# Projection order in a one-layer hybrid decoder step: the fourth delta-net head's columns before the last four gate blocks

## The chip, the cores and the metric

One core of one Trainium2 chip runs the whole step as a single program. The metric is the device time of one execution in microseconds; a comparison takes the median of several runs. Five engines work in parallel, each through its own list of instructions in order: TensorE (PE, with its weight loads shown apart as PEld), VectorE (DVE), ScalarE (ACT), GpSimd (POOL) and SyncE (SP). DMAs are issued by SP and by ACT, from the same in-order lists as their other work.

## What is computed

A hybrid decoder layer for a prompt of 1024 tokens and, beside it, 8 sample tokens with 4096 cached positions each. One input projection (1024 columns of x against 5648 columns of weights) feeds three branches, and a gate:

```python
proj = jnp.dot(h, w['in'])
q_a, k_a, v_a, xbc, dt_raw, qkv_c, beta_raw, a_raw, z = jnp.split(proj, idx, axis=-1)
z_a, z_b, z_c = jnp.split(z, [D_A, D_A + D_B], axis=-1)
...
o_a = (rms_norm(o_a) * w['subln'] * (1 - lam_init)).reshape(b, L, D_A) * jax.nn.silu(z_a)
...
qkv, conv1 = causal_conv(qkv, conv0, conv_w)      # gated delta net, 4 heads of 128
qkv = jax.nn.silu(qkv).astype(f32)
...
o, S1 = gated_delta_chunked(q, k, v, g, beta, S0.astype(f32))
o = (rms_norm(o) * norm_g).reshape(b, L, D_C).astype(z.dtype) * jax.nn.silu(z)
...
out = jnp.dot(jnp.concatenate([o_a, o_b, o_c], axis=-1), w['out'])
```

The branches are differential attention (4 heads), a Mamba-2 scan (SSD) and a gated delta net (4 heads, chunks with a triangular solve each). Everything is float32; the projections are done as three products of rounded high and low parts.

## The kernel before

The projection is feature-major: `proj_fm` (lines 424 to 467) takes a list of items, one for each block of 128 columns. An item is 72 matmuls (three groups `n` of 344 tokens, 24 matmuls each, line 458) into one of three PSUM banks "pj"; after each group the item's `sink` empties the bank. Four kinds of item matter here. A `z_item` (line 980) is a gate block: ACT copies each group into a buffer (line 991), and after every second block both are put through SiLU on ACT and written to DRAM (line 986), to be read again much later. A `g_item` (line 1572) is a third of a delta-net head (its q, its k or its v): `conv_item` (line 953) empties the bank with four DVE operations per group (lines 964 and 969), and after the head's third item the SiLU of all three is recorded and the three buffers are appended to `graw[h]`. An `x_item` does the same for the SSD branch, and a `v_item` is an attention value block.

`groups[3]` (line 1588) lists the 33 items that run in the long middle stretch: four v, head 1's three, four x, head 2's three, four x, twelve z, and last head 3's three. Each long-lived result sits in the pool `up` of 12 buffers of 4 KB per partition (`unit`, line 136): the convolved q, k and v of a head, the z buffers, and inside `gdn_head` the tiles kN, vb, LT, AT, Dm, kb and oC; also attention's kTh (two) and vh.

`gdn_head` (line 1035) is one head: sums of squares, transposes, decay and score blocks for eight chunks (lines 1102 to 1119, the "front"); then the inversion: LT is written to DRAM and read back as Dm by DMAs on ACT's queue (lines 1122 to 1127), 31 dependent pairs of DVE steps (lines 1136 to 1140), the result written and read back again (lines 1143 to 1147); then products and eight sequential state steps (lines 1208 to 1228), and the store. `gdn_all` (line 1601) runs the four heads in turn and yields 0.5 at a time while a head's three buffers are not yet there.

`drive` (line 280) interleaves generators while the program is written: it always advances the one that is furthest behind in its share, by the costs that they yield. The middle stretch is four such drives, cut after 9, 18, 30 and 33 items (`CUTS`); `take` gives the delta net 77% of its cost (`GF`) over them, in proportion to the items. Attention's first loads (`attention_begin`, line 673) are recorded before the last cut's three items. Then the weight pools are closed, and a final `drive` (line 1736) interleaves attention, the rest of the delta net, the SSD scan, the sample steps, the rest of the paged sample attention and the first output weights. The output projection (line 1824) comes last. The program is then scheduled by priority in this recorded order, with the delta net's instructions put forward by 50 places (`OFF`).

Of the kernel before, what the change touches and what calls it, by code (L numbers as in the profile page):

```python
# [87 lines left out]
def trunk_kernel(  # L88
# [47 lines left out]
    def unit(shape, dt=F32, n="u"):  # L136
        return up.tile(shape, dt, tag="u", name=nm(n))
# [807 lines left out]
    def silu_flush():  # L945
        for y, bias, done in late_silu:
            i = act(y, y, AF.Silu, bias=bias)
        exp_ln_tables(i)
        for y, bias, done in late_silu:
            done(y)  # L950
        late_silu.clear()

    def conv_item(c0, wb, ws, ti, tj, done, flush, silu_bias=0.0):
        wv = [vec[:, wb + i * ws + ti:wb + i * ws + ti + 1] for i in range(4)]
        cur = [None]

        def sink(n, ps):
            if n == 0:
                cur[0] = unit([P, T], n="cy")
            y = cur[0]  # L960
            o = 3 if n else 0
            m = CH if n < 2 else CH - NS
            c0_ = n * CH
            V.tensor_scalar_mul(y[:, c0_:c0_ + m], ps[:, o:o + m], wv[3])
            for i in range(3):
                s_ = 0 if n else 3 - i
                q = o - 3 + i + s_
                yv = y[:, c0_ + s_:c0_ + m]
                stt(yv, ps[:, q:q + m - s_], wv[i], yv, ALU.mult, ALU.add)
            if n == 2:  # L970
                V.tensor_copy(tail[:, tj, :], ps[:, o + m - 3:o + m + NS])
                late_silu.append((y, silu_bias, done))
                if flush:
                    silu_flush()

        return (c0, sink, 3)
# [3 lines left out]
    def z_item(j):  # L980

        cur = [None]

        def done(y):
            V.tensor_copy(zS[:, j, :], y[:, T:NTOK])
            S.dma_start(out=zfd[j], in_=y[:, 0:T])

        def sink(n, ps):
            if n == 0:
                cur[0] = unit([P, NTOK], n="zf")  # L990
            S.copy(cur[0][:, n * CH:(n + 1) * CH], ps)
            if n == 2:
                late_silu.append((cur[0], 0.0, done))
                if j % 2:
                    silu_flush()

        return (CZ + j * P, sink, 0)
# [574 lines left out]
    def g_item(h, j):  # L1572
        def done(y):
            graw.setdefault(h, []).append(y)

        return conv_item(CG + 512 * j + h * P, 56, 12, 4 * j + h, 8 + 4 * j + h, done, j == 2)

    def x_item(i):
        def done(y):
            S.dma_start(out=yxd[i], in_=y)  # L1580

        return conv_item(CX + i * P, 16, 8, i, i, done, i % 2 == 1, vec[:, 48 + i:49 + i])
# [4 lines left out]
        [g_item(0, j) for j in range(3)],  # L1587
        [v_item(h) for h in range(4)] + [g_item(1, j) for j in range(3)]
        + [x_item(i) for i in range(4)] + [g_item(2, j) for j in range(3)]
        + [x_item(i) for i in range(4, 8)] + [z_item(j) for j in (4, 5, 6, 7, 0, 1, 2, 3, 8, 9, 10, 11)]  # L1590
        + [g_item(3, j) for j in range(3)],
    ]
    fg = proj_fm([i for g in groups for i in g], lead_w)

# [340 lines left out]
```

## Time and profile before

| | |
|---|---|
| three runs | 1270.9, 1263.82, 1271.76 us; median 1270.9 |
| the profiled execution | 1265.4 us, span 1262.6 us |
| PE busy, weight loads | 1130.7 us (90%), 951.7 us (75%) |
| DVE, ACT, POOL busy | 816.4 us (65%), 477.3 us (38%), 640.6 us (51%) |
| mean granted TensorE clock | 0.951 of full |
| last projection matmul (line 458) | about 839 us |
| first output-projection matmul in a row (line 1824) | 1102 us |

The busy shares are means over stretches with different limits. The middle stretch of projections ends near 839 us, the mixed stretch of the final `drive` lasts from there to about 1092 us, and the output projection takes the rest. The profile's matmul ends are modelled, so PE's busy time and that of its weight loads are both shown.

### The profile page before, as it was taken

What the parts mean: (1) busy time and instruction counts of PE and PEld (TensorE: products, weight loads), DVE (VectorE), ACT (ScalarE), POOL (GpSimd) and SP (SyncE); (2) the same over time, 40 slices, a digit from 0 to 9 for tenths busy, and PEclk for the clock granted to TensorE, in tenths of its full rate; (3) what the DMA queues carried; (4) which work ended last, traced back from release to release, by engine and by line L of the source; (5) the groups of instructions that cost most, each with busy time, mean ns of one, the idle gap of its engine ahead of it and who ended that gap; (6) DMA issues with size and microseconds to landing.
All of it is one profiled execution on the core that took longest, in us unless ns stands there. A gap on an engine that the chain in (4) does not pass through costs nothing.

```text
span 1262.6 us, 22284 instructions
## 1 busy us (share of the span) xinstructions
PE 1130.7 (90%) x7365; PEld 951.7 (75%) x7365; DVE 816.4 (65%) x1945; ACT 477.3 (38%) x1003; POOL 640.6 (51%) x778
## 2 busy tenths in 40 slices
PE   4999999988789989979897899978898999699997
PEld 3799888777668869759776788857577778678876
DVE  5723596538568669953564935786778888664444
ACT  6333224201213532223353243436548658341111
POOL 3757867734567674573865788860023241241100
PEclk9999899998879999999898899989899999899999
DMA  8756676993786882794896699999786564951320
GB/s 287 213 165 194 225 216 195 354 314 94 234 309 218 275 276 81 227 347 155 283 322 204 191 339 330 315 306 228 196 231 187 127 168 137 303 193 63 123 70 34
DMA packets 246451, 275.56 MB, mean 218 GB/s; under 512 B 31905, under 2 KB 163376, under 8 KB 246322
## 3 DMA queue, kind: packets, MB, share of 16 engines
q1 hardware_dynamic: 168082, 214.44, 52.6%
q10 hardware_dynamic: 78256, 59.72, 16.5%
q8 instruction: 58, 0.95, 0.3%
q14 instruction: 55, 0.45, 0.1%
HBM read 231.59 MB, written 42.67 MB: 217 GB/s over the span
## 4 chain that ended last, share of the span: by engine, by line
PE 50%; DVE 17%; DMA 17%; ACT 5%; issue 4%; POOL 3%; SPq 2%; ACTq 1%; DVEq 0%; POOLq 0%
PE b L458 22%; PE b L1824 10%; DVE U L159 4%; PE pv L886 3%; DMA vt<-in_cache_v_dram 3%; DMA w<-in_w_in_dram 3%; DVE cy L167 2%; DVE lg L841 2%; DMA kt<-in_cache_k_dram 2%; POOL kt L840 2%; DMA Dm<-invd 1%; PE b L745 1%; DMA invd<-U 1%; DVE e L721 1%; ACT e L156 1%
## 5 line engine op out<-in xcount | busy, mean ns | idle before, releaser
L458 PE MATMUL b<-hh,whi 128*128 128x344 f32 (+1 forms) x2016 | 506.2, 334 | 22.8 <-DVE cy L167 13.8
L840 POOL TENSOR_TENSOR kt<-kt,qb 128x256 f32<-128x256 f32 x512 | 361.7, 740 | 144.9 <-DMA kt<-in_cache_k_dram 108.7
L458 PEld LDWEIGHTS b<-hh,whi 128*128 128x128 f32 x2016 | 360.2, 195 | 53.8 <-issue 27.7
L458 PE MATMUL b<-hh,wlo 128*128 128x344 f32 (+1 forms) x1008 | 330.7, 333 | 3.5 <-POOL wlo L201 3.4
L841 DVE TENSOR_REDUCE lg<-kt 128x16 f32<-128x1024 f32 x128 | 154.7, 1212 | 95.4 <-POOL kt L840 88.6
L458 PEld LDWEIGHTS b<-hh,wlo 128*128 128x128 f32 x1008 | 196.1, 196 | 15.5 <-issue 10.1
L201 POOL TENSOR_TENSOR wlo<-w,whi 128x512 fp32r<-128x512 f32 x86 | 110.9, 1293 | 89.8 <-ACT whi L155 89.1
L1824 PE MATMUL b<-wo,mh 128*128 128x512 f32 (+1 forms) x408 | 121.8, 380 | 0.0
L155 ACT ACTIVATE whi<-w 128x512 fp32r<-128x512 f32 x86 | 53.8, 630 | 132.6 <-PE b L458 86.7
L167 DVE SCALAR_TENSOR_TENSOR cy<-b,vec,cy 128x341 f32<-128x341 f32 (+4 forms) x180 | 98.9, 564 | 1.3
L886 PE MATMUL pv<-vt,wz 128*32 128x512 f32 x512 | 80.9, 648 | 10.4 <-DMA vt<-in_cache_v_dram 8.5
L1824 PEld LDWEIGHTS b<-wo,mh 128*128 128x128 f32 x408 | 74.7, 188 | 14.1
L1792 POOL TENSOR_TENSOR ml<-zt,mh 128x512 fp32r<-128x512 f32 x16 | 22.4, 1400 | 109.0 <-ACT mh L1791 93.4
L1824 PE MATMUL b<-wo,ml 128*128 128x512 f32 (+1 forms) x204 | 77.2, 378 | 0.0
L155 ACT ACT_TABLE_LOAD x37 | 47.5, 1283 | 26.7 <-POOL wlo L201 7.8
L159 DVE TENSOR_TENSOR U<-U,Dm 128x60 f32<-128x60 f32 (+24 forms) x124 | 43.5, 351 | 17.3 <-DMA Dm<-invd 15.2
L156 ACT ACTIVATE e<-e,nmx 128x128 f32<-128x128 f32 (+7 forms) x64 | 49.1, 768 | 6.7 <-DMA ql<-qfd 2.8
L718 PE MATMUL b<-kTh,qh 128*128 128x128 f32 (+3 forms) x96 | 39.9, 422 | 9.2 <-DVE mx L721 7.2
L159 DVE TENSOR_TENSOR y<-b,gate 128x512 f32<-128x512 f32 (+1 forms) x17 | 11.1, 659 | 54.1 <-PE b L1824 54.1
L1824 PEld LDWEIGHTS b<-wo,ml 128*128 128x128 f32 x204 | 38.4, 188 | 7.3
L159 DVE TENSOR_TENSOR U<-U 128x60 f32<-128x60 f32 (+24 forms) x124 | 41.4, 334 | 2.3
L745 PE MATMUL b<-vh,wT 128*128 128x128 f32 x288 | 40.3, 285 | 1.0 <-ACT wT L738 0.6
(524 smaller groups left out, 1957.2 us busy)
## 6 DMA issues: line engine op xcount, KB each, us to landing
kt<-in_cache_k_dram SPq DMA_DIRECT2D x256, 256.0 KB
vt<-in_cache_v_dram SPq DMA_DIRECT2D x256, 256.0 KB
w<-in_w_in_dram ACTq DMA_DIRECT2D x82, 256.0 KB
zfd<-zf ACTq DMA_DIRECT2D x12, 512.0 KB
wo<-in_w_out_dram SPq DMA_DIRECT2D x12, 512.0 KB
om<-mixd SPq DMA_DIRECT2D x24, 256.0 KB
xt<-in_x_prompt_dram SPq DMA_DIRECT2D x8, 512.0 KB
hx<-in_w_ada_dram SPq DMA_DIRECT2D x16, 256.0 KB
```

The lines of the kernel that those rows point to most:

```text
L155: return S.activation(out, in_, func, bias=bias, scale=scale)
L156: return S.activation(out, in_, func, bias=bias, scale=scale, accum_out=accum)
L159: return V.tensor_tensor(out=out, in0=a, in1=b, op=op)
L167: return V.scalar_tensor_tensor(out=out, in0=a, scalar=s, in1=b, op0=op0, op1=op1)
L201: G.tensor_tensor(out=lo, in0=w32, in1=hi.bitcast(F32), op=ALU.subtract)
L458: TE.matmul(ps[:, 0:N], a, b[k][:, sl], start=(i == 0), stop=(i == 23))
L718: TE.matmul(ps[:, 0:b - a], qh[:, m, ts], kT[m][:, a:b], start=True, stop=False)
L745: TE.matmul(po[:, 0:P], wTs[j // 4][:, j % 4, :], vh[:, j, :], start=(j == 0), stop=(j == i))
L840: G.tensor_tensor(out=kt[:, j, c], in0=kt[:, j, c], in1=qb[:, c], op=ALU.mult)
L841: V.tensor_reduce(out=lg[:, 2 * g:2 * g + 2, :], in_=kt.rearrange("p j (a d) -> p j a d", d=64), axis=AX.X, op=ALU.add)
L886: mm = TE.matmul(pv[32 * r:32 * r + 32, :], wz[:, 2 * g + j, :], vt[:, j, :], start=(b == 0 and g < 2), stop=(b == NS - 1 and g >= 14 and ...
L1824: TE.matmul(ps[c], m[a][:, kt % 4, :], w[kt][:, c[0]:c[1]], start=(kt == KT[0] and i == 0), stop=(kt == KT[-1] and i == 2))
```

## The change

Head 3's three items are moved ahead of the last four gate blocks in the list. Nothing else is touched: the items, their number, the cuts and all shares are the same.

```diff
@@ -1587,8 +1587,8 @@
         [g_item(0, j) for j in range(3)],
         [v_item(h) for h in range(4)] + [g_item(1, j) for j in range(3)]
         + [x_item(i) for i in range(4)] + [g_item(2, j) for j in range(3)]
-        + [x_item(i) for i in range(4, 8)] + [z_item(j) for j in (4, 5, 6, 7, 0, 1, 2, 3, 8, 9, 10, 11)]
-        + [g_item(3, j) for j in range(3)],
+        + [x_item(i) for i in range(4, 8)] + [z_item(j) for j in (4, 5, 6, 7, 0, 1, 2, 3)]
+        + [g_item(3, j) for j in range(3)] + [z_item(j) for j in (8, 9, 10, 11)],
     ]
     fg = proj_fm([i for g in groups for i in g], lead_w)
```

## Rows read from the trace of the kernel before

**Rows 1.** Busy time by stretch: engine busy (instructions), granted clock, DMA share, GB/s.
```profile
core 0: us, PE busy (x) PEld busy (x) DVE busy (x) ACT busy (x) POOL busy (x), PEclk, DMA share, GB/s
735.00:783.00 48.00, 46.39 (x402) 40.20 (x402) 22.82 (x34) 18.20 (x37) 38.53 (x51) 1.00 1.05 345
783.00:839.20 56.20, 55.99 (x369) 48.15 (x367) 41.02 (x79) 24.65 (x36) 44.94 (x59) 1.00 0.97 307
839.20:855.20 16.00, 5.75 (x29) 2.24 (x28) 11.88 (x40) 6.09 (x12) 7.66 (x13) 0.67 1.07 276
855.20:1092.00 236.80, 214.03 (x1494) 172.34 (x1494) 190.33 (x633) 149.78 (x434) 57.47 (x55) 0.95 0.69 190
```

**Rows 2.** Chain of waits before the last projection matmuls: start, us, what.
```profile
810.54 0.22 PE b L1213 x2
810.76 0.22 PE b L1214 x2
810.99 3.98 PE b L458 x25
814.96 0.22 PE b L1218 x2
```

**Rows 3.** PE's weight loads of head 3's front, 839.2 to 882 us.
```profile
L1111 PEld LDWEIGHTS b<-cy 128*128 128x128 f32 x16 | 2.5, 191 | 0.1
L1112 PEld LDWEIGHTS b<-cy,cy 128*128 128x128 f32 x16 | 2.4, 192 | 0.0
L1064 PEld LDWEIGHTS b<-ident,cy 128*128 128x128 f32 x12 | 2.1, 195 | 5.0 <-ACT cy L155 5.0
L1108 PEld LDWEIGHTS b<-rt,s16r 16*128 16x128 f32 x8 | 1.2, 182 | 1.5 <-issue 1.4
```

**Rows 4.** Who waited for whom on PE, 839.2 to 855.2 us: us, times, longest.
```profile
PE b L1064 <- ACT cy L155: 4.5, 1, 4.5
PE b L718 <- DVE mx L721: 3.2, 1, 3.2
PE b L718 <- DVE rz L167: 2.0, 1, 2.0
```

**Rows 5.** ACT in order of time around 850 us.
```profile
852.13 0.58 ACTq L647 DMA_DIRECT2D ql<-qfd  x1
852.74 1.28 ACT L155 ACT_TABLE_LOAD   x1 [3.32 <-DMA ql<-qfd]
854.03 1.06 ACT L155 ACTIVATE cy<-cy 128x1024 f32<-128x1024 f32 x1
855.11 1.28 ACT L186 ACT_TABLE_LOAD   x1
856.40 0.51 ACT L156 ACTIVATE e<-e,nmx 128x256 f32<-128x256 f32 x1
```

**Rows 6.** PE's waits on head 3's own work, 855.2 to 1092 us.
```profile
PE b L736 <- DVE U L159: 1.2, 1, 1.2
PE b L1104 <- ACT em L155: 0.5, 1, 0.5
PE b L1328 <- ACT em L155: 0.5, 1, 0.5
```

**Rows 7.** ACT in order of time where head 2's inversion begins.
```profile
667.71 1.98 ACTq L1124 DMA_DIRECT2D invd<-LT  x4
672.37 1.81 ACTq L1127 DMA_DIRECT2D Dm<-invd  x4
674.22 1.14 ACT L991 COPY zf<-b 128x344 f32<-128x344 f32 x3 [7.00 <-issue]
```

**Rows 8.** PE there: its wait, and the clock after it.
```profile
PE b L458 <- ACT zf L991: 5.9, 1, 5.9
...
675.00:679.00 4.00, 4.00 (x15) 4.00 (x16) 0.00 (x0) 2.71 (x4) 2.80 (x4) 0.50 0.97 273
```

**Rows 9.** Head 3 later: Dm's load on ACT's queue, its DVE steps.
```profile
885.03 0.38 ACTq L1127 DMA_DIRECT2D Dm<-invd  x1
...
L159 DVE TENSOR_TENSOR U<-U,Dm x31: 168/210/1323, 888.8 to 933.0; 128x60 f32<-128x60 f32 x3, 128x28 f32<-128x28 f32 x2, 128x54 f32<-128x54 f32 x2, 128x48 f32<-128x48 f32 x2
```

**Rows 10.** Attention's first loads, head 2's last DMA, the last cut's bank emptying.
```profile
777.16 1.00 ACTq L670 DMA_DIRECT2D bt<-relw  x2
...
787.07 2.72 ACTq L658 DMA_DIRECT2D kTh<-kfd  x4
...
824.93 0.36 ACTq L1229 DMA_DIRECT2D out_dram<-St  x1
...
L964 DVE TENSOR_SCALAR cy<-b,vec x9: 557/566/577, 802.3 to 842.3; 128x344 f32<-128x344 f32 x6, 128x336 f32<-128x336 f32 x3
```

**Rows 11.** Chain of waits at the end of the mixed stretch.
```profile
1076.69 1.16 DVE oA L159
...
1093.66 0.48 ACT ho L1338
```

## Prediction

> **What bounds the kernel now.** I read the busy time by stretch first, then the chain of waits, the waits of PE, and the engines in order of time around the places that the change touches.
>
> The stretches show three regimes [rows 1]. Up to 839.2 us, while the projections run, PE is busy 55.99 of 56.20 us: PE sets the pace, at the full 2.4 GHz level. Then comes a hole: of the 16.0 us from 839.2 to 855.2 PE works 5.75 at a granted clock of 0.67. From 855.2 to 1092 four things are interleaved (attention, the rest of the delta net, SSD, sample work), and PE is busy 214.03 of 236.8 us and DVE 190.33. No one engine is full there, but PE is nearest, with 22.8 us idle. DMA is full until 855 us (share 0.97 to 1.07). The chain of waits before 839 us is projection matmuls with the delta net's small products set between them end to end [rows 2]: what is inserted there lengthens the stretch by its own time.
>
> **What the change does to the recorded order.** The delta net's share of the last cut is 3/33 of 77% of 4 x 89.3, which is 25.0 units. Before, 6 of them go to head 2's last step and end, 16.5 are yields that wait for head 3's columns, and 2.8 record head 3's first pieces (squares and the first transposes). After, head 3's columns are there when head 2 ends, so the same 25 hold 6 for head 2 and 19.4 of head 3: its whole front, the start of its inversion (Dm's loads) and the first three DVE step pairs. In the final drive the head then has 69.9 units left instead of 86.5, of a nominal 90.4: it is done at 77% of that stretch, not at 96%.
>
> **The parts, costed.**
>
> Moved columns: 216 projection matmuls of head 3 go ahead of 288 of the gate blocks. Same matmuls, weight loads and splits, so 0 on PE. Head 3's emptying of banks (36 DVE operations) goes from the stretch 783 to 839.2, where DVE has 41.02 of 56.20 us busy, to the one before, where it has 22.82 of 48.00 [rows 1]; the four gate blocks bring ACT copies in return. Both are covered by PE. Four SiLUs and four stores of 512 KB move some 50 us later on ACT's queue; both places have DMA at 0.97 or more, so I cost that at 0, or at most one store's time, 0.5 MB at 307 GB/s: 1.7 us.
>
> Head 3's front leaves the mixed stretch. Its PE work after 839.2 us, by the weight loads, is 2.5 + 2.4 + 2.1 + 1.2 us and 0.6 in six small ones: 8.8 us [rows 3]. The mixed stretch loses these 8.8 us. But they go into the projections, where pieces lie end to end [rows 2] and PE has 0.2 us to spare [rows 1]: +8.8 there. Sum 0. Bounds: +8.8 if the mixed stretch is held by something else and gives nothing back, -8.8 if the projections swallow the front.
>
> The Trainium skill, page "Perfetto Trace Analysis", section "Identifying the Most-Contended Engine", says that matmul busy time is a poor measure of how full PE is, and that the share of weight loads is a better one. By it PE had 8 us free in 783 to 839.2 us, the front would cost less than a microsecond there, and the sum below would be 8 us lower, about 1260: that is the first term of the first rival. The end-to-end pieces speak against it.
>
> The hole. PE's last wait in it is 4.5 us for the SiLU of head 3's v, which transposes need [rows 4]. That wait goes, since these transposes are done earlier. But what is late next is near: attention's exponentials stand on ACT at 856.40, behind that same SiLU and its two table loads [rows 5], and the last gate blocks put a SiLU in the same place. The other two waits, 3.2 and 2.0 us, are attention's own start, which can't move ahead: its pools open only when the weights' pools close. So the gain is between 0 and 4.5; I take 2.
>
> The inversion starts earlier. Dm's loads are issued at 885.03 and the 31 step pairs run from 888.8 to 933.0 [rows 9]; now they should start near 850, where DVE has idle time and its last convolutions are gone. What that buys at the end: in the mixed stretch PE waits 2.2 us in all for head 3's own DVE and ACT work [rows 6]. From below 0, from above the 22.8 us idle; the nearest row says 2, and I take 2. The end itself is not the head's: after attention's last head at 1076.69 SSD's last output stands at 1093.66 [rows 11].
>
> A new wait. Where head 2's inversion begins, between gate blocks, ACT stands 7.0 us between LT's writes and the loads of Dm [rows 7]; the gate copies queue behind them, PE waits 5.9 us for a bank, and runs the next 4 us at 0.50, the 1.2 GHz level [rows 8]: 5.9 + 2.0 = 7.9 us. Head 3 in its old place had no such copies behind it. In its new place the loads are recorded after the first group of the very last block; only two groups' copies follow, and there are three banks. So between 0 and 7.9; I take 1.
>
> The Trainium skill, page "DMA: Bandwidth & Descriptors", section "Two DMAs through the same engine are not ordered", tells authors to let the issuing engine wait for the first transfer before it issues the dependent one; by that rule ACT must stand here again. The 7.0 us are that wait, and the trace agrees.
>
> Sum: 0 + 0 - 2 - 2 + 1 = -3 us. The profiled execution took 1265.4 (span 1262.6 and 2.8 around it), which gives 1262.4; the runs' median is 5.5 above that execution, and on that scale I predict 1270.9 - 3 = 1268.
>
> **The rivals.**
>
> *The front is free and the head's late chain was holding the end.* The projections absorb the front: -8.8. The hole shrinks by its whole 4.5 us. The head's earlier end lets the last quarter run thinner, some 6 of the 22.8 us idle. Together -19: 1252. For it: DVE is the second fullest engine there, and the front's DVE work leaves it too. Against it: end-to-end pieces, and 2.2 us in [rows 6].
>
> *Slower: the buffers of `up` run out.* Before, at the last cut head 2 holds 6 (q, kN, vb, kb, AT, oC), two gate blocks 2, attention's first loads 3: 11, and head 3's first column block the twelfth. After it is 6 + 3 (head 3's q, k, v) + 1 gate block + 3 = 13, with the next gate block 14. That the pool is tight already is seen: attention_begin records all its loads together, those that need no such buffer go at 777.16 and those that do at 787.07 [rows 10]. If the first block of the last cut finds none, its copy, due where that cut's first group was emptied before (802.3), waits until head 2 gives back five at its last step (824.93) [rows 10]. PE fills the other two banks by about 810 (24 matmuls take 3.8 us by [rows 2]) and stands 15 us, and pays 2 more at the low clock as in [rows 8]: 1270.9 + 17 - 1 = 1287. It decides if head 2 is still two steps from its end when that block comes. Against it: with PE free, head 2's remaining steps would hurry, and attention's loads would give way at little cost.
>
> *The order changes, the times don't.* Head 3's front is recorded early but lands where it was, because head 2 ends late: 1271.
>
> **How the numbers follow.** I give my forecast 0.52 (its own range 1259 to 1277, the front's 8.8 us to either side, which holds the 7.9 of the new wait too), the first rival 0.23, the buffers 0.18, and no effect 0.07. One per cent is 12.7 us, about what a measurement of this kernel can tell from no change: below 1258.2 is faster, above 1283.6 slower. Of the first rival 0.20 lies below, and 0.02 of the forecast: 0.22. Of the buffers 0.16 lies above, 0.02 of the forecast: 0.18. The rest is 0.60. The range leaves about a tenth out on each side: it reaches below the first rival's centre a little and to the buffers' centre: 1249 to 1287.
>
> **What would show it.** After the change the last line-458 matmul should stand near 848 us and not 839; the front's products (lines 1104 to 1112) before it; Dm's loads near 850 and the step pairs ending before 905; the hole after the last projection again some 14 us with the clock down; head 3's last store 30 us or more before SSD's. I am wrong about the front if the last projection matmul is still at 839 to 841; about the new wait if PE waits over 3 us for the gate copies behind Dm's loads; and the buffers decide if gate copies or attention's kTh loads stand until head 2's last step.

## The result, and the profile after

The change made the kernel slower: 1313.0 us (median of four runs, 1311.0 to 1325.4) against 1267.7 for the kernel before in the same session (four runs), a ratio of 1.037 with a 95% interval of 1.033 to 1.041. I had forecast 1268. The profiled execution's span is 1309.2 us; before it was 1262.6, so 46.6 us have to be found. All rows and stretches below are of the one profiled execution of each kernel.

Busy time by stretch, cut at the last projection matmul and at the end of the mixed stretch, which is taken at SSD's last store (1096.6 before, 0.4 us ahead of the cut here, and 1143.7 after; us, then busy time and instructions of PE, PEld, DVE, ACT, POOL; granted clock; DMA share; GB/s). Before:

```profile
700.00:839.30 139.30, 135.70 (x968) 117.83 (x971) 94.19 (x171) 53.03 (x89) 109.14 (x139) 0.98 0.96 307
839.30:1097.00 257.70, 222.49 (x1535) 177.34 (x1535) 204.28 (x679) 159.16 (x456) 65.25 (x69) 0.93 0.72 198
```

After, the same view:

```profile
700.00:866.50 166.50, 152.32 (x1030) 127.95 (x1030) 106.43 (x204) 55.12 (x98) 120.09 (x155) 0.97 0.81 266
866.50:1143.70 277.20, 225.23 (x1476) 177.79 (x1476) 192.99 (x649) 153.43 (x443) 56.93 (x55) 0.88 0.64 180
```

The projections end 27.2 us later, the mixed stretch is 19.5 us longer (19.8 up to the store), the output projection is the same to half a microsecond. In the mixed stretch PE executes 59 matmuls fewer, and yet it is busy longer, at a lower clock, and it stands 52.0 us instead of 35.2.

**The projections.** The table gives, from the starts of the line-458 matmuls in the trace, how long the last 384 of them took (of 3048 in all): 288, in which the change puts most of head 3's columns, and the last 96.

| us | before | after | columns moved, head 3 held back (e1) | front early, inversion held (e2) | score products x4, before (e12) | the same, after (e13) |
|---|---|---|---|---|---|---|
| matmuls 2664 to 2952 | 67.6 | 80.7 | 83.3 | 89.8 | 68.1 | 81.4 |
| the last 96 | 21.6 | 31.4 | 17.8 | 31.4 | 21.6 | 43.4 |

So of the 27.2 us, 13.1 came where the columns went, 9.8 in the last 96 matmuls, where the front went, and 4.3 had gathered before that, 3.7 of it by 619 us, where the two kernels still do the same. The 4.3 need not be the change's: the versions below that keep this beginning and its buffers (all but e5 to e10 and e14 to e16) reach matmul 2664 between 747 and 757 us. Of the 13.1 us, 7.4 are idle time of PE (8.5 us against 1.1); the rest is mostly 16 more matmuls of other work that fell there, and 3.4 us at the 1.2 GHz level. In the last 96, PE is idle in neither kernel.

**The place of the 13.1 us.** The trace in order of time, PE, DVE and ACT of after:

```profile
758.23 0.48 PE L458 MATMUL b<-hh,whi 128*128 128x348 f32 x2
758.79 1.14 PE L1186 MATMUL b<-T,LT 64*64 64x64 f32 x16
...
775.66 0.63 PE L1214 MATMUL b<-St,cy 128*128 128x128 f32 x2
775.94 0.92 PE L458 MATMUL b<-hh,whi 128*128 128x344 f32 x2
...
768.90 0.28 DVE L1225 COPY St<-b 128x128 f32<-128x128 f32 x1
769.09 1.52 DVE L964 TENSOR_SCALAR cy<-b,vec 128x344 f32<-128x344 f32 x3
770.54 0.56 DVE L167 SCALAR_TENSOR_TENSOR cy<-b,vec,cy 128x341 f32<-128x341 f32 x1
...
775.19 1.05 DVE L167 SCALAR_TENSOR_TENSOR cy<-b,vec,cy 128x343 f32<-128x343 f32 x2
...
769.21 0.27 ACT L1226 COPY oC<-b 128x128 f32<-128x128 f32 x1 [1.69 <-DVE St L1225]
```

From 758.9 to 775.9 us there is no projection matmul. All three banks are full with the second of head 3's blocks; its first emptying operations, three at once, come at 769.09, just as head 2's state steps begin (St at 768.90, oC at 769.21), and because the twelve operations of the three groups are interleaved on DVE with other work, the first bank is free only past 775. Before, a gate block stood in that place: no projection matmul for 10.0 us, filled with head 2's products, then three copies on ACT, and PE goes on half a microsecond after they begin:

```profile
764.07 1.15 ACT L991 COPY zf<-b 128x344 f32<-128x344 f32 x3
...
764.58 0.58 PE L458 MATMUL b<-hh,whi 128*128 128x344 f32 x2
```

**The mixed stretch.** ACT in order of time where it starts, after:

```profile
866.01 1.83 ACTq L1124 DMA_DIRECT2D invd<-LT  x4
867.94 1.29 ACTq L647 DMA_DIRECT2D qh<-qfd  x2
870.91 2.69 ACTq L647 DMA_DIRECT2D ql<-qfd  x2
873.66 7.21 ACTq L1127 DMA_DIRECT2D Dm<-invd  x4
880.92 0.40 ACT L156 ACTIVATE e<-e,nmx 128x128 f32<-128x128 f32 x1 [15.40 <-DMA Dm<-invd]
```

ACT stands 15.4 us on DMAs, those of head 3's inversion among them, and attention's first exponential is behind them: it comes 14.4 us after the last projection matmul, before 8.7. Some 5.6 us of it are the twelve issues themselves; the rest is waiting. LT's last write landed at 873.0. Dm's four loads took 0.31 to 0.58 us each to issue, at 873.66, 875.55, 877.85 and 880.56, and each went 0.02 to 0.03 us after one of attention's four q loads had landed (873.64, 875.53, 877.82, 880.54), whose semaphore (the counter that a DMA raises as it lands) it uses again. So ACT stood first for LT's writes and then, 7.5 us long, for attention's own q loads. Then the sample step's last key pages, its value pages, and head 3's inverse, DVE, SP and ACT of after:

```profile
898.98 1.21 DVE L841 TENSOR_REDUCE lg<-kt 128x16 f32<-128x1024 f32 x1
917.14 1.21 DVE L841 TENSOR_REDUCE lg<-kt 128x16 f32<-128x1024 f32 x1
...
930.26 27.87 SPq L821 DMA_DIRECT2D vt<-in_cache_v_dram  x24
...
945.93 6.35 ACTq L1144 DMA_DIRECT2D invd<-U  x4
953.06 0.60 ACT L155 ACTIVATE ems<-b 128x512 f32<-128x512 f32 x1 [7.01 <-DMA invd<-U]
955.32 2.05 ACTq L1147 DMA_DIRECT2D LT<-invd  x4
957.42 0.60 ACT L155 ACTIVATE ems<-b 128x512 f32<-128x512 f32 x1 [3.77 <-DMA ql<-qfd]
961.68 1.66 ACT L1161 COPY T<-b 32x128 f32<-32x128 f32 x6 [3.66 <-PE b L1156]
971.13 0.48 ACT L738 COPY wT<-b 128x384 f32<-128x384 f32 x1 [5.20 <-PE b L745]
```

Before, the last of these reduces was at 849.7 and the value pages were issued from 899 to 924, ahead of the inverse's write (934 to 943). Now they are issued from 930 to 958, the inverse's write and read fall among them, and ACT does next to nothing from 946 to 971. From 958 to 974 us PE runs at or near the half level, 1.2 GHz (the columns are as above; the clock, 0.50 and 0.55, stands behind POOL's):

```profile
958.00:966.00 8.00, 6.32 (x60) 4.80 (x56) 1.39 (x2) 2.29 (x9) 0.00 (x0) 0.50 0.30 101
966.00:974.00 8.00, 8.00 (x76) 4.99 (x69) 0.17 (x1) 1.61 (x5) 0.00 (x0) 0.55 0.00 0
```

### The profile page after: what moved, and what is told of

Read it like the earlier page. It is cut to its first block, busy times and chain, and to the rows that moved or that the text cites. A ratio compares the mean times of both kernels' runs of the same rounds, so it can differ in the third digit from the quotient of the medians.

```text
span 1309.2 us, 22282 instructions
## 1 busy us (share of the span) xinstructions
PE 1152.7 (88%) x7365; PEld 964.4 (74%) x7365; DVE 820.4 (63%) x1945; ACT 474.4 (36%) x1000; POOL 638.6 (49%) x778
## 5 line engine op out<-in xcount | busy, mean ns | idle before, releaser
L458 PE MATMUL b<-hh,whi 128*128 128x344 f32 (+1 forms) x2016 | 505.4, 333 | 23.7 <-DVE cy L167 12.8
L886 PE MATMUL pv<-vt,wz 128*32 128x512 f32 x512 | 80.7, 651 | 14.1 <-DMA vt<-in_cache_v_dram 11.5
L156 ACT ACTIVATE e<-e,nmx 128x128 f32<-128x128 f32 (+7 forms) x64 | 49.1, 770 | 21.9 <-DMA Dm<-invd 15.4
L159 DVE TENSOR_TENSOR U<-U,Dm 128x60 f32<-128x60 f32 (+24 forms) x124 | 44.9, 362 | 16.5 <-DMA Dm<-invd 14.7
L718 PE MATMUL b<-kTh,qh 128*128 128x128 f32 (+3 forms) x96 | 40.3, 428 | 13.1 <-DVE mx L721 7.3
L745 PEld LDWEIGHTS b<-vh,wT 128*128 128x128 f32 x288 | 37.9, 202 | 8.5 <-ACT wT L738 1.8
L745 PE MATMUL b<-vh,wT 128*128 128x128 f32 x288 | 41.8, 291 | 2.3 <-ACT oA L155 1.4
```

The lines of the kernel that those rows point to most:

```text
L156: return S.activation(out, in_, func, bias=bias, scale=scale, accum_out=accum)
L159: return V.tensor_tensor(out=out, in0=a, in1=b, op=op)
L458: TE.matmul(ps[:, 0:N], a, b[k][:, sl], start=(i == 0), stop=(i == 23))
L718: TE.matmul(ps[:, 0:b - a], qh[:, m, ts], kT[m][:, a:b], start=True, stop=False)
L745: TE.matmul(po[:, 0:P], wTs[j // 4][:, j % 4, :], vh[:, j, :], start=(j == 0), stop=(j == i))
L886: mm = TE.matmul(pv[32 * r:32 * r + 32, :], wz[:, 2 * g + j, :], vt[:, j, :], start=(b == 0 and g < 2), stop=(b == NS - 1 and g >= 14 and ...
```

## The experiments

Every ratio is to the kernel before in the same session. "Half level" is the time at which the granted clock stood at 1.2 GHz, worked out microsecond by microsecond from the granted clock; "work" is PE's busy time less half of what was busy at that level, so microseconds at 2.4 GHz (its matmul ends are modelled, so it is good to a few microseconds).

| kernel | median, us | ratio (95%) | last projection matmul | mixed stretch | PE idle there | half level | work |
|---|---|---|---|---|---|---|---|
| before | 1267.7 | 1 | 839 | 257.3 | 35.2 | 37 | 208.9 |
| after | 1313.0 | 1.037 (1.033-1.041) | 866 | 277.1 | 52.0 | 65 | 199.7 |
| e1 columns | 1308.9 | 1.028 (1.022-1.033) | 858 | 279.7 | 46.1 | 57 | 211.0 |
| e2 front | 1301.6 | 1.019 (1.012-1.026) | 872 | 265.3 | 41.8 | 51 | 203.4 |
| e3 loads | 1295.6 | 1.021 (1.013-1.029) | 859 | 268.1 | 48.6 | 51 | 201.3 |
| e4 no tie | 1299.2 | 1.021 (1.015-1.027) | 869 | 262.7 | 45.5 | 38 | 202.5 |
| e5 after, 13+7 | 1307.4 | 1.026 (1.016-1.036) | 870 | 268.9 | 48.0 | 63 | 200.6 |
| e6 before, 13+7 | 1270.4 | 1.004 (0.999-1.008) | 839 | 261.5 | 32.9 | 41 | 211.1 |
| e7 after, 12+7 | 1299.8 | 1.024 (1.013-1.036) | 860 | 272.1 | 47.6 | 61 | 201.1 |
| e8 neutral order | 1272.1 | 0.997 (0.991-1.002) | 841 | 255.9 | 32.6 | 37 | 208.7 |
| e9 after, 11 and oC apart | 1322.3 | 1.042 (1.036-1.048) | 875 | 281.4 | 50.2 | 72 | 201.8 |
| e10 before, the same | 1307.6 | 1.031 (1.023-1.038) | 854 | 291.0 | 46.4 | 79 | 213.8 |
| e12 before, products x4 | 1283.0 | 1.011 (1.005-1.016) | 844 | 274.1 | 36.9 | 47 | 217.9 |
| e13 after, products x4 | 1321.6 | 1.040 (1.032-1.047) | 875 | 279.8 | 47.1 | 85 | 199.1 |
| e14 after, 12 and oC apart | 1321.4 | 1.042 (1.038-1.046) | 883 | 273.1 | 49.5 | 57 | 200.6 |
| e15 before, the same | 1295.5 | 1.025 (1.020-1.029) | 847 | 280.7 | 39.9 | 55 | 216.8 |
| e16 = e14, no tie | 1300.4 | 1.028 (1.024-1.032) | 872 | 258.9 | 38.4 | 40 | 204.4 |
| e17 inversion late | 1302.0 | 1.025 (1.020-1.031) | 875 | 265.5 | 37.3 | 75 | 197.3 |
| e18 after, POOL queue | 1311.5 | 1.031 (1.024-1.038) | 869 | 275.0 | 48.7 | 62 | 202.6 |
| e19 before, POOL queue | 1280.8 | 1.008 (1.004-1.012) | 844 | 270.7 | 42.8 | 50 | 207.9 |

**One part of the change at a time.** A ladder: the columns alone; with the front; with Dm's loads; all of it without one tie. `late` is set when the last projection item has been recorded.

e1:

```diff
-            while len(graw.get(h, ())) < 3:
+            while len(graw.get(h, ())) < 3 or (h == 3 and not late[0]):
```

> The new order of the items, but the delta net is held at the start of head 3 until the last projection item is recorded, as it was before the change: the columns move, head 3's recorded place does not. Before took 1267.7 us, after 1313.0. If the loss comes from head 3's early recording (its inversion, or the tie of the last cached-key reduces to its steps), this run stands near before: 1267 to 1277, and the last line-458 matmul below 850 us. If the moved columns themselves do it (their DVE bank emptying delays weights, PE idle 5.75 of 48 us in 735 to 783 against 1.6), it keeps the 11.7 us of idle in the projections and stands at 1280 to 1300.

1308.9, a ratio of 1.028 where after has 1.037: the larger part of the loss is there without head 3's early recording. The 288 matmuls took 83.3 us, as in after (80.7). So in the projections neither the front nor the inversion is what is lost there. Its mixed stretch is no clean reading of the columns: the hold released head 3 later than before (its first copy ssr stands at 877.6 us, 19 us behind the last projection matmul; before at 833.4, ahead of it), and head 3's last store came at 1126, 12 us before the stretch's end.

e2 (the same hold ahead of the inversion) and e3 (the hold between Dm's loads and the first step):

```diff
+        while h == 3 and not late[0]:
+            yield 0.5
         for b in range(4):
             bsl = slice(32 * b, 32 * b + 32)
             S.dma_start(out=invd[0, h, b]...
```

> As after the change, but head 3 is held ahead of its inversion (the write of LT and the loads of Dm) until the last projection item is recorded; its front may be recorded early. If the early inversion or the tie makes the loss, this is 1268 to 1282: the front costs 13 us or so in the projections and gives 9 back later. If the front itself in the projections is the cause, it stays within 8 us of 1313. The run less e1_columns is the price of the early front alone.

> As after the change, but head 3 is held between the loads of Dm and the first of its 31 step pairs until the last projection item is recorded, so the last cached-key reduces are tied to no step of head 3. If ACT's stand behind Dm's loads at the end of the projections is the loss (15.4 us ahead of the first exponential), this equals after: 1305 to 1316. If the three early step pairs and the tie to them are, it falls to 1285 or below, with the last cached-key reduce (line 841) near 860 us and not at 917.

e2 1301.6, e3 1295.6: neither step alone carries the loss. The last 96 matmuls took 31.4 us in both, as in after: that is the front, not the inversion. I had called e2 less e1 the price of the early front. It is -7.3 us, but not that price: e1 held all of head 3 back, later than before, and e2 carries a wait of its own, a second gap of 10.2 us in the projection matmuls. There DVE stands in one small operation, which in after took 0.36 us; DVE of e2:

```profile
792.76 8.22 DVE L159 TENSOR_TENSOR lg<-lg,fb 128x8 f32<-128x8 f32 x1
```

That is what e2's 89.8 us in the 288 matmuls have above after's 80.7, and e17 has the same 8.22 us at 795.83. In e3 my premise was wrong: the steps were recorded right behind the last item, still ahead of the last key pages, so the tie stayed (reduces at 888 and 904), and the mixed stretch lost 10.8 us against before.

e4, the tie alone (`behind_gdn`, lines 826 to 830, sets the last key pages behind the newest step of the delta net):

```diff
-            gstep[:] = [step.ins]
+            if h < 3:
+                gstep[:] = [step.ins]
...      # the same condition stands before gstep.clear(), ahead of the steps
```

> After the change, with only the tie of the cached-key reduces to head 3's steps taken away (they stay tied to head 2's last step, as they were before in effect). If the tie is what made the mixed stretch 20 us longer (late softmax of the last sample, late value pages, SyncE's queue in order behind them, SSD's chunk inputs 26 us late), this gives 1288 to 1298, the last line-841 reduce stands below 880 us and the fourth load of SSD inputs (line 1270) near 951 us, not 977. If the early inversion itself does it, it stays at 1308 to 1316.

1299.2, a microsecond above what the tie's theory gave, with the last reduce at 865.5 as it said; the fourth load of SSD's inputs came at 965.5, halfway between the 951 that I gave and after's 977. Its key reduces, its value pages on SP, and the mixed stretch:

```profile
L841 DVE TENSOR_REDUCE lg<-kt x4: 1219/1220/1220, 855.2 to 865.5; 128x16 f32<-128x1024 f32 x4
...
918.91 1.48 SPq L821 DMA_DIRECT2D vt<-in_cache_v_dram  x3
923.78 21.99 SPq L821 DMA_DIRECT2D vt<-in_cache_v_dram  x21
...
869.20:1131.90 262.70, 217.18 (x1476) 173.42 (x1478) 190.34 (x647) 153.91 (x443) 55.65 (x56) 0.93 0.69 190
```

The mixed stretch is 14.4 us shorter than after's, with 27 us less at the half level. e16 against e14 repeats it with other buffers: 258.9 against 273.1, 14.2 us. The tie's price is the best repeated number here. The other versions of after fall in line: where the last reduces come early (e2, e4, e16, e17) the mixed stretch is 258.9 to 265.5 us, where they are tied (after, e3, e5, e7, e9, e13, e14, e18) 268.1 to 281.4; e1 stands apart, since it has the front's work back in that stretch.

**The buffers.** e5, e6 and e7 (`NU` long-lived buffers, `NH` half buffers):

```diff
-NU = 12        # e5, e6: 13; e7: 12
-NH = 9         # all three: 7
```

> After the change, with 13 buffers of 4 KB in the pool of long-lived blocks instead of 12, paid for with two of the nine 2 KB half buffers. In the trace of after no projection matmul runs from 758.9 to 776.0 us, and the emptying of the second of head 3's blocks begins only at 769.09, two microseconds after head 2's inverted triangle was read for the last time (766.7). If a missing buffer makes that stall, the thirteenth removes it: against the same kernel with 12 and 7 buffers this run is 6 to 15 us faster, and the gap in the projection matmuls near 760 us falls from 17 to 10 us, as before the change. If it is DVE's or PE's own work there, the two differ by less than 3 us.

> The kernel before with the same 13 and 7 buffers, as a control for the run above. The buffers' theory: before had no such stall, so it stays within 1% of before, 1260 to 1280, and after with 13 and 7 is 25 to 35 us above it instead of 45. If seven half buffers are too few, both rise alike.

> After the change with 12 long-lived buffers as it has, but 7 half buffers: the control for what the two half buffers are worth. Expected 1305 to 1325; the run with 13 less this one is the price of the missing buffer alone.

A thirteenth buffer did not help: 1307.4 with 13, 1299.8 with 12, and the gap stayed (16.9 and 16.5 us). My rival of the buffers falls, in the form of too few of them. Seven half buffers left before as it was (1.004), but after became 13 us faster with them, which I had not expected (projections 6 us, mixed stretch 5 us shorter). It is a warning too: single medians of kernels near after that differ by less than some 10 us say little, and I read the trace's stretches instead.

e8, is any other order as bad?

```diff
-z_item(j) for j in (4, 5, 6, 7, 0, 1, 2, 3, 8, 9, 10, 11)
+z_item(j) for j in (4, 5, 6, 7, 8, 9, 10, 11, 0, 1, 2, 3)
```

> The kernel before with another order of its last twelve gate blocks (4 to 7, 8 to 11, 0 to 3 instead of 4 to 7, 0 to 3, 8 to 11); head 3's columns stay last. No block's kind stands in another place of the list, so nothing that I have named changes: buffers, head 3's place and DVE's emptying are as before. If the losses of the mixed stretch come from what the change does, this is 1260 to 1280. If any other recorded order costs the mixed stretch some 10 to 20 us, it is 1280 or more, and the mixed stretch's part of the loss is not the head's.

No: 0.997, the mixed stretch 255.9. Blocks of one kind can change places; what costs is what the change does.

**Why the block waited.** e9 and e10 (11 shared buffers and one for oC), e14 and e15 (12 and one, with 7 half buffers):

```diff
-        o = unit([P, 8, P], n="oC")
+        o = up.tile([P, 8, P], F32, tag="oC", name=nm("oC"), bufs=1)
```

> After the change, same memory: the pool of long-lived blocks has 11 buffers and the delta net's output block oC has one of its own beside it. A thirteenth buffer changed nothing, and the first emptying operations of the second of head 3's blocks start at 769.09 us, right as head 2's oC gets its first write (769.21). Theory: the pool hands out buffers in the order in which they were asked for in the program; oC was asked for before that block, and gets its buffer only when head 2's state steps begin, so the block's three full banks stand until then, and after that twelve interleaved DVE operations must pass before PE gets a bank. With oC apart the gap of 17 us in the projection matmuls near 760 falls to 5 or less and the last one comes 6 to 12 us earlier than the 866.2 of after: 1301 to 1307 in all. If DVE is held there by the cached-key reduces that wait for POOL, the gap stays above 12 us.

> The kernel before with the same 11 buffers and one for oC. A gate block stands at that place there, with the same wait (10.0 us without projection matmuls from 754.6), but PE fills it with head 2's products and loses under 1 us, and ACT empties the banks with three copies. Theory: the wait costs before nothing, so 1262 to 1272, the same as before. If it gains more than 6 us, the wait for the buffer also held the kernel before, and the change's loss isn't in it.

> After the change with 12 shared long-lived buffers and one of its own for oC beside them, paid for with two half buffers (its control is the run with 12 and 7, 1299.8 us; the 13th shared buffer changed nothing). If the pool's order of requests makes the 17 us gap in the projection matmuls near 760, the gap is gone (5 us or less) and nothing else is short now: 6 to 12 us faster than the control, 1288 to 1295. If the buffers' number is the point, it equals the control within 4 us.

> The kernel before with the same 12 shared buffers and one for oC. Theory: the gap there (10 us from 754.6) was filled with head 2's products, so it gains nothing: 1262 to 1272. If it gains over 6 us, the order of requests held the kernel before too.

At the place itself the theory held: the 17 us gap was gone in e9, e14 and e16 (4.5 us at most there), and the 288 matmuls took 77.7, 72.2 and 73.7 us instead of 80.7. As a whole it failed: e9 and e14 ended at 1322 and 1321, and before lost 29 to 41 us by it (e15, e10), where I had expected nothing. The gap came back later, 15.6 us from 818.5 in e9 and 17.0 from 847.2 in e14, with head 2's last steps and head 3's first pieces in it. Nor was the gap all that the columns cost: with the same buffers the old order took 63.6 (e10) and 65.6 us (e15) for the 288 matmuls, so without the gap the new order is still 14.1 and 6.6 us behind. So a block asked for behind oC waits for oC; but taking oC out of that order lets other things slip, and PE's total idle time from 700 us to the last projection matmul did not fall (17.2 and 22.6 us, after 14.2). No version here gains by it.

> As the run with 12 shared buffers and one for oC, and the tie of the last cached-key reduces to head 3's steps taken away too. In the trace of after the tie puts the last 24 value pages at 930 to 958 us, on top of the write and read of head 3's inverse (945.9 to 957.4 on ACT's queue), and ACT works about 4 of the 25 us from 946 to 971. Theory: both savings add: 1274 to 1284. If they overlap, it equals the better one alone, 1290 to 1299.

1300.4, 21 us below e14. In the mixed stretch the tie's saving is the same with oC apart (14.2 us); e16's projections also ended 11.7 us earlier than e14's, which the tie does not explain. Since e14 itself saved nothing, the sum I gave did not come.

**What PE's work is worth in either place.** e12 (before) and e13 (after) repeat head 3's score products:

```diff
+                for _ in range(3 if h == 3 else 0):
+                    TE.matmul(kq[:, i * 256:i * 256 + P], kT[:, cs], kT[:, cs], start=True, stop=True)
+                    TE.matmul(kq[:, i * 256 + P:i * 256 + 256], kT[:, cs], qT[:, cs], start=True, stop=True)
```

> The kernel before, with the 32 score products of head 3's front (lines 1111 and 1112, 4.9 us by their weight loads) done four times over: 14.7 us more of PE work early in the mixed stretch. If PE's work there lengthens the stretch one for one, as my sum had it when it let 8.8 us leave, this costs 11 to 16 us: 1280 to 1286. If the front falls there into PE's gaps, so that taking it out gives nothing back, it costs 0 to 6 us: 1267 to 1274.

> After the change, with the same score products of head 3 four times over: now the 14.7 us stand among the last projection matmuls. If the projections swallow nothing, it costs 13 to 16 us against after (1326 to 1329) and the last line-458 matmul stands 13 to 16 us after 866.2. If PE's sequence there has room by the weight loads, it costs less than 8.

e12 cost 16.0 us by the medians (some 13 by the ratio of 1.011), about one for one: work in the early mixed stretch does count. By the table it is not work alone: the mixed stretch grew by 16.8 us, 9.0 of work, 6.2 more at the half level and 1.7 of idle time. e13 stretched the last 96 matmuls from 31.4 to 43.4, 12.0 us for 14.7 of work; its median is 8.6 above after's, less than the 13 to 16 that I had given. In the projections, too, nearly nothing is swallowed. That is the place for the Trainium skill's page "Perfetto Trace Analysis", section "Identifying the Most-Contended Engine", by whose weight-load share the front would have been almost free there: here the measurement decides against reading a free share of weight loads as room.

**Who holds the mixed stretch.** e17 keeps the front early and puts the inversion back:

```diff
+        while h == 3 and not late[0]:
+            yield 0.5
...
+                if i >= 4:
+                    late[0] = 1     # in attention(): its fifth piece is recorded
```

> After the change, but head 3 waits ahead of its inversion (write of LT, loads of Dm) until attention's first head has recorded its fifth piece, about where the inversion stood before the change. The front stays among the projections, 12 buffers as in after. Theory: ACT's stand for Dm's loads at attention's start and for the inverse's round trip under the value pages is what took back the front's 9 us; without them the mixed stretch is 244 to 254 us (before 257, after 277), and with some 22 us more in the projections the whole takes 1278 to 1290. If the mixed stretch stays at 262 or more, something else holds it, and the whole is above 1294.

1302.0, and a mixed stretch of 265.5: by the bounds that I had set, the theory falls. The row of the mixed stretch in e17 shows where:

```profile
875.40:1140.90 265.50, 228.21 (x1474) 184.04 (x1475) 191.51 (x647) 153.91 (x442) 56.51 (x55) 0.86 0.67 187
```

PE's idle time is back, 37.3 us against 35.2 before, and its work is 11.6 us below before's. But the clock is 0.86: 75 us at the half level instead of 37. Stretch = work + idle + what the half level adds: 197.3 + 37.3 + 30.9 = 265.5; before 208.9 + 35.2 + 13.2 = 257.3. So in this execution the idle time and the work came as the theory had them, and what they gave back was eaten by the clock. That is weaker than it looks. The execution took 1309.7 us at a mean clock of 0.928; the other three took 1292.0 to 1302.7 us at 0.938 to 0.945, and their mixed stretches are not known. And DVE's 8.22 us, told at e2, put 10.2 us into its projections, which the theory did not count. So e17 does not decide who holds the mixed stretch.

e18 and e19 issue the inversion's four DMA steps from POOL:

```diff
-            S.dma_start(out=invd[0, h, b]...
+            Q.dma_start(out=invd[0, h, b]...      # Q = G for head 3; so too for the other three steps
```

> After the change, with the four DMA steps of head 3's inversion (write of LT, load of Dm, write and read of the inverse) issued by GpSimd instead of ACT; all else as in after. In after's mixed stretch PE does 9 us less work than before, as I had predicted, but stands 16.8 us more and runs 27.7 us longer at the 1.2 GHz level. Theory: it is ACT's list that makes both, since attention's exponentials stand behind these DMAs, 15.4 us at attention's start and most of 946 to 971. Then the first exponential comes 8 us or less after the last projection matmul (14.7 in after), PE's idle time in the mixed stretch falls from 52 to 42 or less and the stretch from 277 to 255 to 266: 1290 to 1302 in all. If the late steps of head 3 themselves are what PE waits for, it stays at 1308 to 1318.

> The kernel before with the same four DMA steps on GpSimd's queue: the control. Before, ACT issued Dm's loads in 1.6 us with no stand, 45 us into the mixed stretch. Theory: nothing to gain, 1260 to 1272. If GpSimd's queue itself helps or costs, it shows here, and e18 is read against it.

In e18 the first exponential came 2.9 us after the last projection matmul, as expected, and yet the whole stayed at 1311.5. The tie is still in it, and between 930 and 980 us PE stands on the value pages itself:

```profile
PE pv L886 <- DMA vt<-in_cache_v_dram: 9.8, 4, 4.4
```

So ACT's list alone is not what holds PE there. But e19, the kernel before with these steps on POOL, is 12.8 us above it by the medians, some 10 by the ratio (1.008); so e18 can be "no gain", or a gain of that size that the queue took back. This stays open.

## Why the prediction was wrong, step by step

**The front: right.** I had 8.8 us leave the mixed stretch and enter the projections. PE's work in the mixed stretch fell by 9.2 us (208.9 to 199.7), and the last 96 projection matmuls took 9.8 us more (31.4 against 21.6), in e2, e3, e4 and e17 as well. The end-to-end pieces of [rows 2] were read rightly, and e13 confirms them.

**The moved columns: wrong, the first large miss.** I costed them at 0, since DVE had more room in the stretch that they moved to [rows 1] and PE would cover the emptying. They cost 13.1 us (e1: 15.7), 7.4 of it idle time of PE. The busy shares hid two things. A gate block's bank is free after one ACT copy, a block of head 3 after four DVE operations, and when three full banks wait together, the twelve are interleaved. And they do wait together: at that place the block gets no buffer until oC has its own. How much of the 13.1 us is this wait is not shown: with oC apart the gap went, and 6.6 to 14.1 us against the old order with the same buffers stayed. Room on an engine says nothing of when a block may start. My largest figure, one store's 1.7 us, was for another resource.

**The hole: no gain where I had 2.** The SiLU of [rows 4] is gone as foreseen, but PE works 5.5 us of the first 16, before 5.75, and attention starts later, not earlier.

**The new wait: right place, wrong queue before and behind it.** I asked what is queued behind Dm's loads on ACT, as in [rows 7], and took gate copies: at most 7.9 us, taken as 1. What stood behind them was attention's first exponential, 5.7 us later than before, and what stood between LT's writes and Dm's loads were attention's q loads, for which ACT waited too. The Trainium skill's page "DMA: Bandwidth & Descriptors", section "Two DMAs through the same engine are not ordered", has the issuing engine wait for the first transfer before it issues the dependent one. The traces agree, with less time than I gave it: of the 7.0 us of [rows 7], 3.8 are the eight issues and 2.7 lie between them (669.7 to 672.4); of the 15.4 us here, what came behind LT's landing at 873.0 is the q loads'. What the late exponential costs in all is not shown: in e4 and e16 it is as late (14.6 and 13.8 us after the last projection matmul), and their mixed stretches, 262.7 and 258.9, are shorter than e2's 265.3, where it comes after 2.9.

**The earlier inversion: wrong sign, the second large miss.** I had it gain 2. The steps, [rows 9] 888.8 to 933.0, ran from 889.2 to 944.8, in 55.6 us instead of 44.2. What the sum left out is who is tied to these steps. `behind_gdn` puts the last key pages behind the newest recorded step, and by recording three step pairs early the change made that head 3's step instead of head 2's, long done. Counted from the last projection matmul, the inverse's write came at 79 us instead of 95, and the value pages at 64 to 91 instead of 60 to 85: they met. Taking only the tie away puts the pages at 50 to 77 and returns 14.4 us of the mixed stretch, and 14.2 in the second pair.

**The sum.** Of the 46.6 us: 4.3 stood already when the changed part began, where versions differ by up to 10, 13.1 are the columns, 9.8 the front, 19.8 the mixed stretch (less work 9.2, more idle 16.8, more half level 12.3, rounded), and the output projection took 0.5 less. Of the mixed stretch's time the tie explains 14; of its 16.8 us of idle time 6.5 went with the tie (e4), and nearly all with the inversion put back, where the tie is gone too (e17). In e4 the half level went back to 38 us with the tie (before 37). What lowers the clock is not settled beyond that: idle time and half level rise together from before to after (35 and 37 to 52 and 65), but e4 has 45.5 us of idle time at before's half level, and e17's execution before's idle time with 75 us at the half level. By the forecast's own terms, then, the step that failed first is the moved columns at 0 (measured 13.1), and with it the earlier inversion at -2, whose tie cost 14; the front's two terms came as computed.

**The rivals.** "Front free" falls (e12, e13). "Buffers run out" had the right sign, and attention's first loads that need such a buffer came later, as it said (kTh at 803 us, [rows 10] 787; vh at 815), but the number of buffers was not it (e5 against e7). "The times don't change" falls with the result.

## What to carry to other kernels

Before moving work past other work, ask of each moved piece what it needs to start: who asked for a buffer before it in a shared pool, how many operations free its bank, and which other instructions are tied to "the latest" of something that the move makes earlier. A busy share shows that an engine has room, not that the work can use it. And price a stretch in three parts, work, idle time and clock: here the work moved as computed, and the other two lost three times as much.

## What the hardware showed that I had not expected

The half level alone cost the mixed stretch 12.3 us in after and 17.7 in e17's execution, against before, with less work to do; in e17 with only 2 us more idle time. A DVE operation of 128x8 that took 0.16 us in before and 0.36 in after at that place took 8.22 us in e2 and in e17, and both times it ended within 0.03 us of the end of an unbroken run of POOL's operations (in e2 at 800.99 and 800.96); it is the same operation on both sides, so its own size does not explain it. Four loads of Dm, 0.31 to 0.58 us each to issue, took 7.21 us from the first to the last on ACT's list, because each stood until an earlier load of the same list had landed; with nothing of the kind ahead of them they took 1.8 at 672.37 [rows 7]. And the same four DMA steps issued from POOL made the kernel before some 10 us slower by the ratio (e19: 1.008, 1.004 to 1.012), though POOL works only 65 us of the mixed stretch's 257.
